# The MLP's down projection: three blocks turned by VectorE and DMA, the fourth summed feature by feature

## The chip, the cores and the metric

The kernel runs on one NeuronCore of a Trainium2 chip. The metric is the device time of one execution in microseconds. The five engines have queues of their own: TensorE (PE in the profile; its weight loads are PEld), VectorE (DVE), ScalarE (ACT), GpSimd (POOL) and SyncE (SP), from whose queue nearly all DMAs are issued.

## The reference, cut to what matters

The model is a decoder of two layers over 256 positions with 2048 features. Each layer has a mixer (dilated attention in layer 0, sparse attention in layer 1), an MLP, and a gated embedding; each works on a normed copy of the residual stream `h` and adds to it. What the change touches is the MLP and the norm that reads its result:

```python
for i in range(DEPTH):
    ...
    hn = rmsnorm(h, mlp_norm_g[i])
    h = h + jnp.square(jax.nn.relu(hn @ mlp_w1[i])) @ mlp_w2[i]
    gate = jax.nn.sigmoid(rmsnorm(h, ple_norm_g[i]) @ ple_w_gate[i])
    h = h + (p[i] @ ple_w_proj[i]) * gate
return rmsnorm(h, final_norm_g)
```

`mlp_w1` is 2048 x 8192 and `mlp_w2` is 8192 x 2048, both float32.

## The kernel before, in words

**Layout.** The residual stream lies in SBUF feature by feature: sixteen tiles `x[k]` of 128 features by 256 tokens, which are the halves of eight tiles `xp[j]` of 128 x 512. Each operand of a product is kept as a rounded part and the rest (`hi`, `lo`), and a product is hi x hi + hi x lo + lo x hi. An activation tile (`xa`, `h`) holds its two parts side by side, 128 x 512.

**Weights come in chunks** of 128 x 1024 float32 (512 KB), one DMA each on SP's queue into one of four `raw` buffers. ScalarE rounds a chunk into `whi` (L227), VectorE subtracts to get `wlo` (L235; six and five buffers), and TensorE uses both. `Program.run` writes this order out: for each chunk it issues the load up to seven chunks ahead, the two splits three to four chunks ahead, then advances every unfinished step by one piece, and then issues the chunk's matmuls. A step is a Python generator; each `yield` puts its next piece behind the next chunk's splits, and `yield "tensor"` behind the next chunk's matmuls. So all engines' queues are fixed in program order.

**Two kinds of product.** `quad` computes four tiles of 128 features, feature by feature: a chunk is 16 matmuls (L366 with 512 columns, weights' rounded part against both parts of the activation; L368 with 256 columns, weights' rest against the rounded part), into four PSUM banks, for which two rings of four (`mm` and `at`) take turns. `token_major` computes 512 features of all tokens, token by token: a chunk is 12 matmuls of 512 columns (L456), into two banks.

**The MLP** (`mlp`) runs over four blocks (`NFB`) of 2048 hidden features. In each, four quads make the hidden tiles `h` (up projection, with the norm's factor, relu and square), then four calls of `token_major`, a quarter (512) of the 2048 output features each, make the block's part of the down projection. `down` sums these parts over the blocks in `y`, token by token: ScalarE copies the first block (L518), VectorE adds the others (L516). After the fourth block's quarter, eight transposes on TensorE (L527) turn the quarter back to feature by feature, in two PSUM banks, behind the next chunk's matmuls; VectorE adds the two banks to `xp` (L531); and `renorm` makes the next norm's activation tiles and its sum of squares.

**After the MLP** comes `ple`: a projection of `p` (one chunk, quad over `pg`), then a quad of the gate over the activation tiles `xa` that `renorm` made, four times in turn. The norm's factor is a hook behind the gate's fifth chunk.

**A bounce** (`bounce`) exists for mixer A: VectorE turns a tile in blocks of 32 x 32 (L867), a DMA writes it to DRAM (L180), and four DMAs read it back with blocks moved (L184), which together is a full transpose; the reads wait for the write on SP's queue.

`add_to_x` adds both halves of a quad's PSUM bank to `x[k]` (L489, L490); `out_proj`, the projection behind each mixer, uses it already.

Of the kernel before, what the change touches and what calls it, by code (L numbers as in the profile page):

```python
# [10 lines left out]
F32 = mybir.dt.float32  # L11
# [4 lines left out]
P = 128  # L16
D = 2048
T = 256
# [10 lines left out]
NFB = 4  # L29
# [9 lines left out]
G_ATTN, G_MLP, G_PLE, G_KV, G_FIN = 0, 2, 4, 6, 7  # L39
# [105 lines left out]
def kernel(ctx: ExitStack, tc: tile.TileContext, a: dict, out: bass.AP):  # L145
    nc = tc.nc
    ctx.enter_context(tc.manual_schedule())
    prog = Program()
# [10 lines left out]
    cur = {}  # L159

    def open_pool(key):
        es = ExitStack()
        cur[key] = es.enter_context(tc.tile_pool(name=key, reuse_waits="tile", bufs=1))
        cur[key + "/es"] = es

    def close_pool(key):
        cur.pop(key)
        cur.pop(key + "/es").close()
# [4 lines left out]
    def bounce(src, name, to):  # L173

        m = src.shape[1] // 4
        d = dpool.tile([P, 4 * m], F32, tag=name, name=name, bufs=2)
        nc.sync.dma_start(d, src)  # L180
        yield
        d4 = d.rearrange("(a s) (b n) -> b s a n", a=4, b=4)
        for b in range(4):
            nc.sync.dma_start(to[32 * b:32 * b + 32], d4[b])  # L184
# [8 lines left out]
    xp = [xg0[:, :2 * T]] + [xpool.tile([P, 2 * T], F32, name=f"x{j}") for j in range(1, KT // 2)]  # L193
# [151 lines left out]
    def renorm(k, gi, to, norm):  # L345

        t = split_hi(k, gi)
        s = norm.square(k)
        yield
        split_lo(t, k, gi)  # L350
        to[k] = t
        norm.add(s)
# [76 lines left out]
    def two_banks(mm):  # L429
        if mm:  # L430
            return [bank(), bank()]
        b = banks2()
        return [b[:, 0, :], b[:, 1, :]]
# [54 lines left out]
    def add_to_x(k, ps):  # L488
        nc.vector.tensor_add(x[k], ps[:, :T], x[k])  # L489
        nc.vector.tensor_add(x[k], ps[:, T:], x[k])  # L490
# [15 lines left out]

    def mlp(layer, xg, norm, to, norm2):

        def down(b, q, ps0, ps1, mm):
            c = slice(q * 512, (q + 1) * 512)  # L510
            if b == q == 0:
                cur["y"] = cur["h"].tile([P, 2, D], F32, name=f"y{layer}")
            y = cur["y"]
            for j, ps in enumerate((ps0, ps1)):
                if b:
                    nc.vector.tensor_add(y[:, j, c], ps, y[:, j, c])  # L516
                else:
                    nc.scalar.copy(y[:, j, c], ps)  # L518
            if b < NFB - 1:
                return  # L520
            yield
            yield "tensor"
            tr = two_banks(not mm)
            for f in range(4):
                for j in range(2):
                    k = 4 * q + f
                    nc.tensor.transpose(tr[f // 2][:, (f % 2 * 2 + j) * P:(f % 2 * 2 + j + 1) * P],  # L527
                                        y[:, j, k * P:(k + 1) * P], ident)
            yield
            for i in range(2):  # L530
                nc.vector.tensor_add(xp[2 * q + i], tr[i], xp[2 * q + i])  # L531
            for i in range(2):
                yield
                both = [renorm(4 * q + 2 * i + f, G_PLE + layer, to, norm2) for f in range(2)]
                for g in both:
                    next(g)
                yield
                for g in both:
                    next(g, None)

        for b in range(NFB):
            h = [None] * 16
            for q in range(4):
                def done(f, ps, q=q, h=h):
                    t = sum_halves(ps)
                    yield
                    while norm.r is None:
                        yield
                    nc.vector.scalar_tensor_tensor(t, t, 0.0, norm.rb, op0=ALU.max, op1=ALU.mult)
                    yield  # L550
                    nc.scalar.activation(t, t, AF.Square)
                    ht = cur["h"].tile([P, 2 * T], F32R, tag="h", name="h", bufs=20)
                    yield from split_to(ht, t)
                    h[4 * q + f] = ht
                base = layer * 128 + (b * 4 + q) * 8
                quad(lambda c, base=base: a["w1"][base + c], KT, xg, done,
                     {4: [norm.factor]} if b == 0 and q == 0 else None, late=True,
                     twos=() if q else (0,) if b else (5,) if layer else ())
            for q in range(4):
                base = layer * 128 + (b * 4 + q) * 8  # L560
                token_major(lambda c, base=base: a["w2"][base + c], h,
                            lambda ps0, ps1, mm, b=b, q=q: down(b, q, ps0, ps1, mm), whole=True)

    def load_p(layer, to):
        for k in range(2):
# [7 lines left out]
    def ple(layer, pg, xg, norm, nxt, norm2, last):  # L573
        pj = [None] * KT
# [158 lines left out]
        for q in range(4):  # L733
            def proj_done(f, ps, q=q):
                s = tmp.tile([P, T], F32, tag="es", name="es", bufs=4)
                nc.scalar.copy(s, ps[:, :T])
                t = cur["h"].tile([P, T], F32, tag="pj", name="pj", bufs=8)
                nc.vector.tensor_add(t, ps[:, T:], s)
                pj[4 * q + f] = t
                return  # L740
                yield
            if q == 3 and last:
                pt = {}

                def pt_done(j, ps):
                    pt[j] = f32(cur["h"].tile([P, 2 * T], F32R, tag="h", name="h", bufs=20))
                    nc.scalar.copy(pt[j], ps)
                    return
                    yield
                parity[0] ^= 1  # L750
                token_major(lambda c: a["w_proj"][layer * 4 + q], pg, pt_done,
                            ring=bank if parity[0] else banks2, kt=2)
                last_quad(pt)
                return
            if q == 2 and last:
                prog.op(load_gain)
            quad(lambda c, q=q: a["w_proj"][layer * 4 + q], 2, pg, proj_done, twos=() if q else (0,))
            hooks = {4: [norm.factor]} if q == 0 else {}
            if q == 3 and not last:
                for c in range(6):  # L760
                    hooks[c] = [lambda k=k: split_x(k, G_KV, nxt) for k in (2 * c, 2 * c + 1)]
            quad(lambda c, q=q: a["w_gate"][layer * 32 + q * 8 + c], KT, xg,
                 lambda f, ps, q=q: gate_done(4 * q + f, ps), hooks)
# [206 lines left out]
    def start1():  # L970
        while x_kv[KT - 1] is None or n_b1.r is None:
            yield
        close_pool("h")
        open_pool("O")
        kvt["o0"] = cur["O"].tile([P, 2 * T], F32R, tag="ob", name="ob", bufs=HB // 2)
        for g in range(GB):
            kvt["k", g] = k_tile()
        open_pool("B")
        pb = cur["B"]
        value_tiles("vs", pb)  # L980
        kvt["vc"] = pb.tile([P, GB * DH], F32R, name="vc")
        nc.gpsimd.memset(f32(kvt["vc"]), 0.0)
        kvt["m0"] = pb.tile([P, P], F32, name="m0")
        kvt["m1"] = pb.tile([P, T], F32, name="m1")
        kvt["mc"] = pb.tile([P, 2, 2, 16], F32, name="mc")
        nc.gpsimd.dma_start(kvt["m0"], a["mB0"])
        nc.gpsimd.dma_start(kvt["m1"], a["mB1"])
        nc.gpsimd.dma_start(kvt["mc"], a["mC"])
        kvt["gs"] = pb.tile([P, 2, 64], F32, name="gs")
        for j in range(2):  # L990
            kvt["pc", j] = pb.tile([P, P], F32R, name=f"pc{j}")
            kvt["pcT", j] = pb.tile([P, T], F32R, name=f"pcT{j}")
            for n in ("pc", "pcT"):
                nc.gpsimd.memset(f32(kvt[n, j]), 0.0)
        for n in ("w2_k", "w2_v"):
            zt[n] = pb.tile([P, 2, DH], F32, name=n)
            nc.gpsimd.dma_start(zt[n], a[n])
        for n in ("rcC", "rcS"):
            zt[n] = pb.tile([64, 32], F32, name=n)
            nc.gpsimd.dma_start(zt[n], a[n])  # L1000
        open_pool("C")
        pc = cur["C"]
        for n in ("rk", "rv"):
            zt[n] = pc.tile([P, GB * T], F32, name=n)
        for j in range(2):
            zt["z", j] = pc.tile([P, 8, 2, GB, 16], F32R, name=f"z{j}")
            nc.gpsimd.memset(f32(zt["z", j]), 0.0)
        for n in ("pe_k", "pe_v"):
            zt[n] = pc.tile([P, 32], F32, name=n)
            nc.gpsimd.dma_start(zt[n], a[n])  # L1010
# [388 lines left out]
    ple(1, p1, x_p1, n_p1, None, n_fin, True)  # L1399

    prog.run(load, copy, sub)
    close_pool("h")


# [108 lines left out]
```

## Time and profile before

| | |
|---|---|
| median of 3 runs | 2495.51 us (2495.19 to 2495.7) |
| the profiled execution: time | 2495.55 us |
| the profiled execution: span from first to last instruction | 2493.8 us |
| mean granted TensorE clock | 0.999 |
| PE / DVE / ACT busy | 2482.9 / 1663.7 / 1345.3 us |
| weight chunks split on VectorE (L235) | 875, of 1.22 us each |
| mean DMA rate | 191 GB/s |

A row of the groups gives a source line, an engine, the operation with what it writes and reads, how often, then busy us and the mean ns of one. A row of the waits gives who waited for whom: us in all, times, and the longest. A row of the chain gives start, length and what ran. "L527" is line 527 of the kernel before; in the changed kernel the lines behind the edit are some 17 higher.

### The profile page before, as it was taken

How to read it: one execution, taken by the hardware profiler on the slowest of the kernel's cores; microseconds unless marked ns; L12 is line 12 of the kernel's file. 1: busy time of each engine (PE TensorE's matmuls, PEld its weight loads, DVE VectorE, ACT ScalarE, POOL GpSimd, SP SyncE). 2: the span in 40 equal slices, each digit the busy share in tenths (PEclk: the TensorE clock that was granted, in tenths of full speed). 3: DMA queues.
4: the chain of work that ended last, by engine and by line, in shares of the span. 5: the costliest groups of instructions: out<-in, count | busy, mean ns of one | idle time of the engine just before them, and what ended most of it. 6: DMA issues, size and time to landing. Idle time of an engine off the chain costs nothing.

```text
span 2493.8 us, 35888 instructions
## 1 busy us (share of the span) xinstructions
PE 2482.9 (100%) x13349; PEld 2138.5 (86%) x13349; DVE 1663.7 (67%) x2818; ACT 1345.3 (54%) x2162; POOL 10.4 (0%) x24
## 2 busy tenths in 40 slices
PE   9999999999999999999999999999999999999998
PEld 8888888888888888888888889988888888888887
DVE  7866686865565565556788989776546556556676
ACT  6444444554454453555665788655545445445465
POOL 0000000000000000000000000000000000000000
PEclk9999999999999999999999999999999999999999
DMA  8566566555556656655565743465555555665553
GB/s 276 193 224 205 194 208 202 178 189 192 194 187 193 194 192 192 191 190 187 187 196 187 254 153 125 142 194 186 194 192 188 194 194 187 194 194 188 185 186 131
DMA packets 136110, 475.80 MB, mean 191 GB/s; under 512 B 15296, under 2 KB 19840, under 8 KB 135936
## 3 DMA queue, kind: packets, MB, share of 16 engines
q1 hardware_dynamic: 134832, 471.66, 58.2%
q8 instruction: 104, 1.70, 0.3%
q0 software_dynamic: 528, 1.07, 0.1%
q10 hardware_dynamic: 576, 0.79, 0.1%
q14 instruction: 70, 0.57, 0.1%
HBM read 467.69 MB, written 5.77 MB: 190 GB/s over the span
## 4 chain that ended last, share of the span: by engine, by line
PE 99%; DMA 0%; ACT 0%; issue 0%; DVE 0%; SPq 0%; ACTq 0%; DVEq 0%
PE mm L366 23%; PE mm L456 18%; PE at L366 17%; PE at L456 17%; PE mm L368 11%; PE at L368 8%; PE at L841 1%; PE at L1348 0%; PE mm L1372 0%; PE mm L1104 0%; PE mm L1105 0%; PE mm L598 0%; PE mm L600 0%; PE mm L599 0%; PE at L1298 0%; DMA raw<-in_w_v 0%
## 5 line engine op out<-in xcount | busy, mean ns | idle before, releaser
L235 DVE TENSOR_TENSOR wlo<-raw,whi 128x1024 fp32r<-128x1024 f32 (+1 forms) x875 | 1065.6, 1219 | 631.6 <-PE at L456 131.5
L227 ACT CAST whi<-raw 128x1024 fp32r<-128x1024 f32 (+1 forms) x875 | 919.1, 1051 | 877.7 <-PE mm L456 198.7
L366 PE MATMUL mm<-xa,whi 128*128 128x512 f32 x2208 | 755.2, 395 | 0.0
L368 PE MATMUL mm<-xa,wlo 128*128 128x256 f32 x2208 | 575.4, 278 | 0.0
L366 PE MATMUL at<-xa,whi 128*128 128x512 f32 x1632 | 568.3, 394 | 0.0
L366 PEld LDWEIGHTS mm<-xa,whi 128*128 128x128 f32 x2208 | 399.3, 188 | 76.1 <-issue 0.4
L368 PE MATMUL at<-xa,wlo 128*128 128x256 f32 x1632 | 453.1, 278 | 0.0
L368 PEld LDWEIGHTS mm<-xa,wlo 128*128 128x128 f32 x2208 | 414.9, 188 | 20.3
L366 PEld LDWEIGHTS at<-xa,whi 128*128 128x128 f32 x1632 | 306.1, 188 | 70.3
L456 PE MATMUL at<-whi,h 128*128 128x512 f32 x1024 | 315.8, 390 | 0.0
L456 PE MATMUL mm<-whi,h 128*128 128x512 f32 x1024 | 315.6, 390 | 0.0
L368 PEld LDWEIGHTS at<-xa,wlo 128*128 128x128 f32 x1632 | 306.7, 188 | 0.1
L456 PEld LDWEIGHTS at<-whi,h 128*128 128x128 f32 x1024 | 192.0, 188 | 39.6
L456 PEld LDWEIGHTS mm<-whi,h 128*128 128x128 f32 x1024 | 191.6, 188 | 39.5
L456 PE MATMUL at<-wlo,h 128*128 128x512 f32 x512 | 199.4, 389 | 0.0
L456 PE MATMUL mm<-wlo,h 128*128 128x512 f32 x512 | 199.3, 389 | 0.0
L456 PEld LDWEIGHTS mm<-wlo,h 128*128 128x128 f32 x512 | 96.1, 188 | 20.0
L456 PEld LDWEIGHTS at<-wlo,h 128*128 128x128 f32 x512 | 96.1, 188 | 19.9
L456 PE MATMUL mm<-whi,xa 128*128 128x512 f32 x320 | 98.9, 390 | 0.0
L374 DVE TENSOR_TENSOR et<-mm,es 128x256 f32<-128x256 f32 x137 | 55.7, 421 | 61.6 <-ACT es L372 59.7
L372 ACT COPY es<-mm 128x256 f32<-128x256 f32 x137 | 48.4, 371 | 68.8 <-PE mm L368 65.8
L456 PEld LDWEIGHTS mm<-whi,xa 128*128 128x128 f32 x320 | 59.7, 188 | 12.2
(331 smaller groups left out, 2131.1 us busy)
## 6 DMA issues: line engine op xcount, KB each, us to landing
raw<-in_w SPq DMA_DIRECT2D x512, 512.0 KB, 3.5
raw<-in_w_qk SPq DMA_DIRECT2D x96, 512.0 KB, 3.6
raw<-in_w_gate SPq DMA_DIRECT2D x64, 512.0 KB, 3.8
raw<-in_w_kv SPq DMA_DIRECT2D x48, 512.0 KB, 4.1
raw<-in_w_v SPq DMA_DIRECT2D x47, 512.0 KB, 4.4
raw<-in_w_q SPq DMA_DIRECT2D x32, 512.0 KB, 4.3
raw<-in_w_oB SPq DMA_DIRECT2D x32, 512.0 KB, 3.5
raw<-in_w_oA SPq DMA_DIRECT2D x16, 512.0 KB, 3.4
```

The source lines that it names most:

```text
L227: nc.scalar.copy(hi[:, c], t[:, c])
L235: nc.vector.tensor_sub(lo[:, c], t[:, c], f32(hi)[:, c])
L366: nc.tensor.matmul(ps, hi[:, col:col + P], rhs, start=first, stop=False)
L368: nc.tensor.matmul(ps[:, :T], lo[:, col:col + P], rhs[:, :T], start=False, stop=last)
L372: nc.scalar.copy(s, ps[:, :T])
L374: nc.vector.tensor_add(t, ps[:, T:], s)
L456: nc.tensor.matmul(st[j], *parts[j][i], start=k == i == 0, stop=k == kt - 1 and i == 2)
L841: nc.tensor.matmul(sb[:, j, T + (g - 1) * P:T + g * P] if g else sb[:, j, :T], q[:, own], k[:, own] if g else k, start=True, stop=True)
```

## The change

The sums of the first three blocks still grow in `y`, which is now two tiles, one for each half of the 2048 features. When the third block's second quarter of a half is added, VectorE turns the half in blocks of 32, one instruction of 128 x 1024 for each 128 tokens, into tiles `z` of a pool of their own. Two DMAs write these to DRAM and eight read them back into a tile `yw`, feature by feature, during the rest of the third block and the fourth block's up projection. Four adds of 128 x 512 on VectorE put the half into `xp`. The fourth block's down projection is four quads, whose results `add_to_x` adds to `x`, and `renorm` follows. The transposes on TensorE and the adds from their banks are gone. The pool `z` is closed behind the MLP, and a pool `j` for the tiles `pj` of `ple` is opened in its place. Both layers are changed alike.

```diff
     def mlp(layer, xg, norm, to, norm2):
+        prog.op(lambda: open_pool("z"))
+        y = {}
+
         def down(b, q, ps0, ps1, mm):
-            c = slice(q * 512, (q + 1) * 512)
-            if b == q == 0:
-                cur["y"] = cur["h"].tile([P, 2, D], F32, name=f"y{layer}")
-            y = cur["y"]
+            half, c = q // 2, slice(q % 2 * 512, (q % 2 + 1) * 512)
+            if b == 0 and q % 2 == 0:
+                y[half] = cur["h"].tile([P, 2, D // 2], F32, tag="y", name="y", bufs=2)
             for j, ps in enumerate((ps0, ps1)):
                 if b:
-                    nc.vector.tensor_add(y[:, j, c], ps, y[:, j, c])
+                    nc.vector.tensor_add(y[half][:, j, c], ps, y[half][:, j, c])
                 else:
-                    nc.scalar.copy(y[:, j, c], ps)
-            if b < NFB - 1:
+                    nc.scalar.copy(y[half][:, j, c], ps)
+            if b < NFB - 2 or q % 2 == 0:
                 return
-            yield
-            yield "tensor"
-            tr = two_banks(not mm)
-            for f in range(4):
-                for j in range(2):
-                    k = 4 * q + f
-                    nc.tensor.transpose(tr[f // 2][:, (f % 2 * 2 + j) * P:(f % 2 * 2 + j + 1) * P],
-                                        y[:, j, k * P:(k + 1) * P], ident)
-            yield
-            for i in range(2):
-                nc.vector.tensor_add(xp[2 * q + i], tr[i], xp[2 * q + i])
-            for i in range(2):
+            zs = []
+            for j in range(2):
                 yield
-                both = [renorm(4 * q + 2 * i + f, G_PLE + layer, to, norm2) for f in range(2)]
-                for g in both:
-                    next(g)
+                z = cur["z"].tile([P, D // 2], F32, tag="z", name="z", bufs=2)
+                nc.vector.transpose(z.rearrange("p (b t r) -> p t b r", b=4, r=32),
+                                    y[half][:, j].rearrange("p (t b s) -> p t b s", b=4, s=32))
+                zs.append(z)
+            w = cur["h"].tile([P, 8, T], F32, tag="y", name="yw", bufs=2)
+            yield
+            moves = [bounce(z, "dM", w[:, 4 * j:4 * j + 4]) for j, z in enumerate(zs)]
+            for g in moves:
+                next(g)
+            for g in moves:
                 yield
-                for g in both:
-                    next(g, None)
+                next(g, None)
+            yield
+            for n in range(4):
+                yield
+                xn = xp[4 * half + n].rearrange("p (f a r) -> p f a r", f=2, r=32)
+                wn = w.rearrange("p a (t r) -> p t a r", r=32)[:, 2 * n:2 * n + 2]
+                nc.vector.tensor_add(xn, wn, xn)
...
             for q in range(4):
                 base = layer * 128 + (b * 4 + q) * 8
-                token_major(lambda c, base=base: a["w2"][base + c], h,
-                            lambda ps0, ps1, mm, b=b, q=q: down(b, q, ps0, ps1, mm), whole=True)
+                if b < NFB - 1:
+                    token_major(lambda c, base=base: a["w2"][base + c], h,
+                                lambda ps0, ps1, mm, b=b, q=q: down(b, q, ps0, ps1, mm), whole=True)
+                    continue
+
+                def done(f, ps, q=q):
+                    add_to_x(4 * q + f, ps)
+                    yield
+                    yield from renorm(4 * q + f, G_PLE + layer, to, norm2)
+                quad(lambda c, base=base: a["w2"][base + c], 16, h, done, late=True)
+        prog.op(lambda: close_pool("z"))
+        prog.op(lambda: open_pool("j"))
...
-                t = cur["h"].tile([P, T], F32, tag="pj", name="pj", bufs=8)
+                t = cur["j"].tile([P, T], F32, tag="pj", name="pj", bufs=8)
...
+        close_pool("j")
         close_pool("h")
```

More of the change, by code (lines that the diff above doesn't have):

```diff
@@ L1401 @@
     prog.run(load, copy, sub)
+    close_pool("j")
     close_pool("h")
```

## The prediction

> **What bounds the kernel now.** I read the head of the page first, then the waits of TensorE, then the chain of waits in order of time.
>
> ```profile
> span 2493.8 us, 35888 instructions
> ...
> PE 2482.9 (100%) x13349; PEld 2138.5 (86%) x13349; DVE 1663.7 (67%) x2818; ACT 1345.3 (54%) x2162; POOL 10.4 (0%) x24
> ...
> PEclk9999999999999999999999999999999999999999
> ...
> PE 99%; DMA 0%; ACT 0%; issue 0%; DVE 0%; SPq 0%; ACTq 0%; DVEq 0%
> ```
>
> TensorE (PE) fills the span, at an even granted clock; the chain that ends last is 99% PE. The waits view with TensorE alone says the same more sharply:
>
> ```profile
> PE mm L772 <- DVE ones L196: 1.1, 1, 1.1
> PE at L273 <- DVE acc L264: 1.0, 1, 1.0
> PE at L456 <- ACT whi L227: 0.5, 2, 0.3
> ```
>
> In the whole run PE waited 2.6 us, in four places. So the time is the sum of what PE issues, and a change counts by what it does to PE's own stream plus any wait that it brings back. VectorE (67%) and ScalarE (54%) matter only if they come so late that PE waits.
>
> **What PE pays for the fourth block now.** The chain in order of time (start, length, what) has the second layer's blocks:
>
> ```profile
> 2004.00 21.76 PE at L456 x96
> 2114.51 21.77 PE mm L456 x96
> ...
> 2290.30 21.77 PE mm L456 x96
> 2312.08 5.44 PE at L456 x24
> 2318.39 16.34 PE at L456 x72
> ```
>
> A quarter of the down projection, token by token, is 96 matmuls of 512 columns in 21.76 us: 227 ns each, 8 chunks of 2.72 us. Between the end of one block's last quarter (2004.00 + 21.76 = 2025.76) and the next block's first (2114.51) lie 88.75 us: the up projection's 4 quads of 8 chunks, feature by feature, so 22.19 us a quad, 2.773 us a chunk of 16 matmuls (8 of 512 and 8 of 256 columns). In the fourth block there is a hole after 24 matmuls: 2312.08 + 5.44 = 2317.52, and the next piece starts at 2318.39. These 0.87 us are the eight transposes of one quarter:
>
> ```profile
> L527 PE MATMUL mm<-ident,y 128*128 128x128 f32 x32 | 4.1, 272 | 0.0
> L527 PE MATMUL at<-ident,y 128*128 128x128 f32 x32 | 4.1, 272 | 0.0
> ```
>
> ```profile
> 2379.89 0.62 PE L366 MATMUL mm<-pg,whi 128*128 128x512 f32 x2
> ...
> 2382.66 0.40 PE L366 MATMUL at<-xa,whi 128*128 128x512 f32 x1
> ...
> 2385.44 1.03 PE L527 MATMUL mm<-ident,y 128*128 128x128 f32 x8
> 2386.23 0.47 PE L366 MATMUL at<-xa,whi 128*128 128x512 f32 x1
> ```
>
> The first pair are two lines of the groups, 64 transposes in all, so 8 groups of 8 over both layers. The second is PE's timeline at the end of the second layer's MLP: the last group, behind the gate's first chunk, holds PE from 2385.44 to 2386.23, 0.79 us, and 0.87 with the slower restart that the hole in the chain includes.
>
> **Part by part. Removed from PE:** 8 groups of transposes, 8 x 0.87 = 6.96 us (8 x 0.79 = 6.3 as the lower bound). They lie on the bound itself, so all of it is gained.
>
> **Changed on PE:** the fourth block's four quarters become quads: 32 chunks a layer at 2.773 instead of 2.72 us, 64 x 0.053 = +3.4 us. The products are the same number of columns (12 x 512 = 8 x 512 + 8 x 256 = 6144); four more matmuls a chunk cost the difference. No quad with h as its moving side is in this trace; the nearest rows are the quads over xa (2.773) and the one over pg, 2382.66 - 2379.89 = 2.77. So the bounds are 0 (the pace of the down projection) and 3.8 us (64 x 0.06); I take 3.4, since two sorts of quads agree.
>
> The Trainium skill, "TensorE: Matmul & The Clock Gate", section Back-to-back issue gap, gives N/2.4 + 2.5 ns between matmuls; by it 512 columns would be 215.8 ns, and the exchange would cost an estimated 0.6 us. The trace disagrees: 227 ns, and 0.053 us a chunk.
>
> **Removed from and added to VectorE.** The groups of its instructions (busy, mean ns):
>
> ```profile
> L235 DVE TENSOR_TENSOR wlo<-raw,whi 128x1024 fp32r<-128x1024 f32 x871 | 1062.9, 1222 | 631.0 <-PE at L456 131.5 <-PE mm L456 130.0 <-PE mm L368 123.7
> ...
> L516 DVE TENSOR_TENSOR y<-mm,y 128x512 f32<-128x512 f32 x24 | 16.5, 692 | 9.1 <-PE mm L456 9.1
> ...
> L867 DVE STREAM_TRANSPOSE zA<-p 128x1024 f32<-128x1024 f32 x7 | 8.7, 1246 | 0.2
> ...
> L489 DVE TENSOR_TENSOR x<-mm,x 128x256 f32<-128x256 f32 x16 | 6.7, 416 | 0.0
> ...
> L531 DVE TENSOR_TENSOR x<-mm,x 128x512 f32<-128x512 f32 x8 | 5.2, 687 | 6.0 <-PE mm L527 6.0
> L799 DVE TENSOR_TENSOR p<-p,oT 128x512 f32<-128x512 f32 x7 | 4.8, 686 | 0.0
> ```
>
> A layer loses 8 sums into y (8 x 0.69 = 5.5 us) and 8 adds of the turned quarter (8 x 0.69 = 5.5). It gains 4 turns of 128x1024 (the turn in mixer A is this very instruction: 4 x 1.25 = 5.0), 8 adds of 512 from the returned tile (8 x 0.69 = 5.5, by the nearest add of two SBUF tiles) and 32 adds of 256 from PSUM (32 x 0.42 = 13.4). Net +12.9 us a layer. Where it lands:
>
> ```profile
> 917.70:1004.70 87.00, 87.00 (x386) 72.12 (x385) 46.65 (x49) 37.38 (x43) 0.00 (x0) 1.00 0.60 193
> 1004.70:1093.50 88.80, 88.80 (x513) 77.66 (x513) 53.26 (x71) 46.49 (x70) 0.00 (x0) 1.00 0.59 190
> 1093.50:1183.30 89.80, 89.80 (x411) 74.64 (x410) 58.69 (x78) 46.17 (x67) 0.00 (x0) 1.00 0.59 188
> ```
>
> These are windows of layer 0: the third block's down projection, the fourth block's up and its down projection (length, then busy PE, PEld, DVE, ACT, POOL; clock, DMA share, GB/s). VectorE is busy 46.65 of 87, 53.26 of 88.8, 58.69 of 89.8 us. With two turns and four adds more (5.2) in each of the first two, and about 58.69 - 11.0 + 13.4 = 61 in the third, it stays under 70%. Cost to the end: nothing, as long as its lead over PE lasts.
>
> That lead:
>
> ```profile
> DVE wlo L235 <- PE at L456: 131.5, 88, 1.8
> ...
> ACT pt L877 <- DMA wA<-dA: 7.7, 7, 1.6
> ```
>
> VectorE keeps waiting for PE to give a wlo buffer back; there are five, so it starts the split of a chunk when four chunks still lie ahead of it: 4 x 2.72 - 1.22 = 9.7 us between a wlo that is ready and PE's use of it. A stall of VectorE under 9.7 us is not seen by PE.
>
> **Added DMAs and waits.** Per half of the features: two writes of 512 KB to DRAM, then eight reads of 128 KB, all on SP's queue between weight loads. Both sorts exist in mixer A; the two lines' answers (with the landing of each) and the weights' row:
>
> ```profile
> L180 SPq DMA_DIRECT2D dA<-zA x7: 326/327/331, 101.6 to 386.9; - x7
> ...
> DMA to landing us min/median/max: 2.6/3.5/5.0
> ```
>
> ```profile
> L184 SPq DMA_DIRECT2D wA<-dA x28: 325/424/852, 104.5 to 393.2; - x28
> ...
> DMA to landing us min/median/max: 2.6/4.0/5.0
> ```
>
> ```profile
> raw<-in_w SPq DMA_DIRECT2D x512, 512.0 KB, 3.5
> ```
>
> Two waits are new. SP's reads wait for the writes to land, and weight loads stand behind them. VectorE's first add of the half waits for the reads, and the splits of weights stand behind that. In the program the first add comes four chunks after the writes, 4 x 2.72 = 10.9 us. The moves take, by the longest landing of each leg in series (write, write, read, read), 4 x 5.0 = 20 us; by room on the queues: 193 GB/s at a share of 0.60 is 322 at full share, 129 to spare, and 2.1 MB there and back take 16 us. So VectorE stands 0 to 9 us at that add, likeliest about 5, against a lead of 9.7: PE waits 0. The two halves are 16 chunks (44 us) apart and VectorE is idle a third of that, so the lead is back before the second. The single bounce in mixer A agrees: its reader waited 7.7 us in seven times, and PE has no row for it.
>
> The Trainium skill, "VectorE: DVE Perf Modes", section Rules for kernel authors, speaks against the change: for a 128x128 transpose it names TensorE, if PSUM will do as the target. Here the trace decides by which engine is full: each turn moved is 0.87 us off PE per 1.25 on an engine that idles a third of the time; kept to the rule, the sum would be +3.4 us for the quads alone.
>
> **The sum.** -6.96 + 3.4 = -3.6 us. The profiled execution took 2495.55 us (span 2493.8 and 1.75 around it); 2492.0 would be its time. The median of the three runs, 2495.51, lies 0.04 below it; so 2491.9 to 2492.0, -0.14%. A measurement of this kernel can tell about 0.2% (5 us) from no change, so this counts as the same.
>
> **Rivals.**
>
> *PSUM comes back late at the gate (same).* Now the last quarter's two banks are read at once; in the changed kernel the last quad fills a ring of four, two features' adds are put off by a chunk, and after one chunk (the projection of p) the gate wants this ring.
>
> ```profile
> 2380.09 1.29 DVE L516 TENSOR_TENSOR y<-at,y 128x512 f32<-128x512 f32 x2 [1.44 <-PE at L456]
> 2381.29 1.22 DVE L235 TENSOR_TENSOR wlo<-raw,whi 128x1024 fp32r<-128x1024 f32 x1
> 2382.42 1.41 DVE L738 TENSOR_TENSOR pj<-mm,es 128x256 f32<-128x256 f32 x4
> ```
>
> VectorE follows PE by 0.20 us here (2379.89 to 2380.09). From the end of the last quad: the first two features' four adds (0.42 each) from -1.39 + 0.2 on, when their half of the chunk is done, over at 0.5; a split, 1.7; the other two features' four adds, 3.4. PE asks for the third bank at 2.77 + 1.39 = 4.2. That is 0.8 us to spare. One split more ahead of them costs 0.4 a layer (2492.8), the four pj adds as well 1.9 (2495.7).
>
> *The bounce outlasts the lead (slower).* It decides from moves of 10.9 + 9.7 = 20.6 us on. Half as long again as 16 us is 24.5: VectorE stands 13.6, PE waits 3.9 in each of four halves, 15.7 us: 2507.7. For it: two bounces at once, in runs of 1 KB, beside full weight traffic, which no row shows. Against it: mixer A's 1.1 us a bounce.
>
> *The quads cost nothing extra (faster).* If the 2.773 belonged to the up projection's busier VectorE and not to its matmuls, the whole 6.96 would be won: 2488.6, -0.28%. The page's gap rule gives nearly this. Against it: the chunk over pg has none of that work and takes 2.77 too.
>
> **Chances.** Forecast 0.78 (its own range 2491.4 to 2493.0, by 6.3 to 7.0 off and 3.4 to 3.8 on), late PSUM 0.07, bounce 0.08, free quads 0.07. Faster: 0.07 and 0.01 for what I have not seen. Slower: 0.08 and 0.01. Same: 0.83. The range leaves out the bounce and the free quads, 0.15; it goes up to the late PSUM's 2495.7, and down to half of the free quads, 2495.5 - 6.96 + 1.7 = 2490.3.
>
> **What would show it.** In the profile after: no transposes between the fourth block's quarters; quads of 22.19 us there, and about 177.5 us from the start of its up projection to the projection of p; a turn of about 1.25 us; PE's waits still under 3 us. A PE row naming wlo with VectorE idle on a DMA from dM would prove the bounce; a PE row naming x at the gate's first chunk, the late PSUM; a fourth-block quad of 21.8, the free quads.

## The result and the profile after

The changed kernel takes 2491.78 us (median of 22 runs, 2491.26 to 2493.05), the kernel before beside it on the same chip 2495.3 (22 runs, 2495.03 to 2495.7). The ratio is 0.9986 [0.998, 0.9992]: 3.5 us less, which by 0.2% counts as the same time. The profiled execution of after is its slowest, 2493.05 us (span 2491.3); where that matters it is said.

The head of the page after, its shares of the chain, and the waits view with TensorE alone (us in total, times, longest):

```profile
span 2491.3 us, 36361 instructions
...
PE 2479.3 (100%) x13541; PEld 2144.3 (86%) x13541; DVE 1682.9 (68%) x2874; ACT 1344.8 (54%) x2162; POOL 10.3 (0%) x24
...
PE 97%; DMA 1%; DVE 1%; ACT 0%; issue 0%; SPq 0%; ACTq 0%; DVEq 0%
```

```profile
PE mm L1139 <- ACT et L1133: 1.1, 1, 1.1
PE mm L789 <- DVE ones L196: 1.1, 1, 1.1
PE at L273 <- DVE acc L264: 1.0, 1, 1.0
PE at L456 <- ACT whi L227: 0.4, 1, 0.4
```

TensorE is as full as before. Of its four rows three stood there before (2.6 us); the first row is new and lies far from the change, in the second layer's compression stage (its matmul starts at 1436.4 us). No row names `wlo`, and none names `x` at the gate.

Now the part that was changed. First the chain of before in order of time (start, length, what): the last quarter of the third block's down projection, and the two matmuls of L297 that stand right ahead of the second projection of p, behind the MLP, in layer 0 and then in layer 1. Below it the same places of after, with the start of the first projection of p (2378.54).

```profile
983.37 21.76 PE at L456 x96
...
1210.04 0.43 PE mm L297 x2
...
2179.80 21.76 PE at L456 x96
...
2406.45 0.43 PE mm L297 x2
```

```profile
983.53 21.76 PE at L456 x96
...
1208.21 0.43 PE mm L297 x2
...
2179.28 21.76 PE at L456 x96
...
2378.54 0.46 PE mm L366 x2
...
2403.97 0.43 PE mm L297 x2
```

From the end of the third block to the second projection of p, before takes 1210.04 - 1005.13 = 204.91 us in layer 0 and 2406.45 - 2201.56 = 204.89 in layer 1; after takes 1208.21 - 1005.29 = 202.92 and 2403.97 - 2201.04 = 202.93. That is -1.99 and -1.96, together -3.95 us. Most of the rest of the difference lies between the two layers: from 1210.04 to 2179.80 before has 969.76 us, and from 1208.21 to 2179.28 after has 971.07. The 1.31 us given back there are the new wait of 1.1 us and little else. The median run is 1.27 us faster than the profiled one; that it lacks most of this wait fits the number, but only the slowest run was profiled, so it is not shown.

VectorE's groups of after (busy us, mean ns, idle before), the two kinds of adds, the sums into `y` and the turns:

```profile
L490 DVE TENSOR_TENSOR x<-mm,x 128x256 f32<-128x256 f32 x32 | 13.6, 425 | 1.1
...
L546 DVE TENSOR_TENSOR x<-yw,x 128x512 f32<-128x512 f32 x16 | 11.0, 687 | 14.6 <-DMA yw<-dM 8.4 <-DMA raw<-in_w 6.1
...
L521 DVE TENSOR_TENSOR y<-mm,y 128x512 f32<-128x512 f32 x16 | 10.8, 690 | 4.5 <-PE mm L456 4.5
...
L530 DVE STREAM_TRANSPOSE z<-y 128x1024 f32<-128x1024 f32 x8 | 9.9, 1237 | 0.0
```

And the three windows of layer 0 that the prediction costed (length, busy PE, PEld, DVE, ACT, POOL, clock, DMA share, GB/s):

```profile
917.70:1004.70 87.00, 87.00 (x387) 72.08 (x386) 50.79 (x56) 37.52 (x43) 0.00 (x0) 1.00 0.68 218
1004.70:1093.50 88.80, 88.80 (x513) 77.63 (x512) 57.13 (x77) 46.16 (x69) 0.00 (x0) 1.00 0.66 214
1093.50:1182.30 88.80, 88.80 (x515) 77.68 (x514) 61.05 (x94) 46.28 (x67) 0.00 (x0) 1.00 0.57 190
```

VectorE went from 46.65, 53.26 and 58.69 us to 50.79, 57.13 and 61.05. The DMA share rose by 0.07 to 0.08 where the moves run. None of it reached TensorE.

The first move in time: SyncE's queue and VectorE's timeline (start, length, instruction, in brackets what it stood for):

```profile
966.89 1.10 SPq L180 DMA_DIRECT2D dM<-z  x2
...
972.48 1.76 SPq L184 DMA_DIRECT2D yw<-dM  x4
...
974.76 1.85 SPq L184 DMA_DIRECT2D yw<-dM  x4
```

```profile
983.07 0.69 DVE L546 TENSOR_TENSOR x<-yw,x 128x512 f32<-128x512 f32 x1 [3.67 <-DMA yw<-dM]
```

From the issue of the writes to the first add are 983.07 - 966.89 = 16.2 us. VectorE stood 3.67 us, with the next split of weights behind it, and TensorE did not notice.

### The profile page after: what moved, and what is told of

Its sections match the earlier page's. It is cut to its first block, busy times and chain, and to the rows that moved or that the text cites. A ratio compares the mean times of both kernels' runs of the same rounds, so it can differ in the third digit from the quotient of the medians.

```text
span 2491.3 us, 36361 instructions
## 1 busy us (share of the span) xinstructions
PE 2479.3 (100%) x13541; PEld 2144.3 (86%) x13541; DVE 1682.9 (68%) x2874; ACT 1344.8 (54%) x2162; POOL 10.3 (0%) x24
## 4 chain that ended last, share of the span: by engine, by line
PE 97%; DMA 1%; DVE 1%; ACT 0%; issue 0%; SPq 0%; ACTq 0%; DVEq 0%
PE mm L366 25%; PE at L366 19%; PE mm L456 15%; PE mm L368 12%; PE at L456 11%; PE at L368 10%; DMA raw<-in_w_kv 1%; PE at L858 1%; DVE wlo L235 1%; PE at L1366 0%; PE mm L1390 0%; PE mm L615 0%; PE mm L617 0%; PE mm L616 0%; PE at L1316 0%
## 5 line engine op out<-in xcount | busy, mean ns | idle before, releaser
L456 PE MATMUL mm<-whi,h 128*128 128x512 f32 x768 | 236.5, 389 | 0.0
L456 PE MATMUL at<-whi,h 128*128 128x512 f32 x768 | 236.4, 389 | 0.0
L456 PEld LDWEIGHTS at<-whi,h 128*128 128x128 f32 x768 | 144.2, 188 | 29.9
L456 PEld LDWEIGHTS mm<-whi,h 128*128 128x128 f32 x768 | 143.7, 188 | 29.8
L456 PE MATMUL mm<-wlo,h 128*128 128x512 f32 x384 | 149.4, 389 | 0.0
L456 PE MATMUL at<-wlo,h 128*128 128x512 f32 x384 | 149.4, 389 | 0.0
L366 PE MATMUL at<-h,whi 128*128 128x512 f32 x256 | 88.9, 394 | 0.0
L366 PE MATMUL mm<-h,whi 128*128 128x512 f32 x256 | 88.9, 394 | 0.0
L456 PEld LDWEIGHTS mm<-wlo,h 128*128 128x128 f32 x384 | 72.1, 188 | 15.0
L456 PEld LDWEIGHTS at<-wlo,h 128*128 128x128 f32 x384 | 72.1, 188 | 15.0
```

The costliest lines, as they stand in the source:

```text
L366: nc.tensor.matmul(ps, hi[:, col:col + P], rhs, start=first, stop=False)
L456: nc.tensor.matmul(st[j], *parts[j][i], start=k == i == 0, stop=k == kt - 1 and i == 2)
```

## The experiments

The theory: the time is TensorE's own stream, transposes taken away and quads put in; the moves and VectorE's extra work cost nothing because VectorE's splits lie some 10 us ahead. The rivals: the moves cost something that the transposes pay for; the two terms have other sizes and meet by chance; the lead or the room at the gate's PSUM is far from its end, or already past it. Where a trace is compared below, "the stretch" is the one measured above, from the end of the third block to the second projection of p: 204.91 and 204.89 us before, 202.92 and 202.93 after.

**No moves.** After without the turns, the DMAs and the adds from `yw`:

```diff
-            if b < NFB - 2 or q % 2 == 0:
-                return
-            zs = []
...
-                nc.vector.tensor_add(xn, wn, xn)
+            return
+            yield
```

> The changed kernel without the turns on VectorE, the DMAs to DRAM and back and the adds from the returned tile (the three blocks' sums never reach x); TensorE's instructions are those of the changed kernel. If the bounce is wholly hidden, as the prediction holds: the changed kernel's 2491.8 us, within 0.5. If the bounce costs TensorE a wait somewhere, also later by a thinner lead: faster than 2491.8 by that wait, 1 us or more.

Measured: 2491.99 us (11 runs, 2491.25 to 2492.49), ratio to before 0.9986 [0.9977, 0.9995], the ratio of after itself. In its trace the stretch takes 202.93 us in both layers (1208.25 - 1005.32 and 2403.07 - 2200.14), as in after to 0.01. 8 turns, 8 writes, 32 reads and 16 adds cost nothing that shows: they are hidden.

**No transposes.** Before without the transposes and the adds of the turned quarters:

```diff
-            tr = two_banks(not mm)
-            for f in range(4):
-                for j in range(2):
...
-                    nc.tensor.transpose(...)
...
-                nc.vector.tensor_add(xp[2 * q + i], tr[i], xp[2 * q + i])
```

> The kernel before without the eight groups of transposes on TensorE and the adds of the turned quarters (the MLP's sum never reaches x); renorm stays. By the prediction's first term (0.87 us a group) 2495.3 - 7.0 = 2488.3; by the pieces of the two traces, where a group with its slow restart costs 0.90, 2488.1. If the transposes were partly covered by something else: 2490 or more.

Measured: 2488.36 us (7 runs, 2488.01 to 2489.24), ratio 0.9972 [0.9961, 0.9983]. That is -6.95 us by the medians. In its trace the stretch takes 201.22 us in both layers, 7.36 less than before in all.

**Quads alone.** Before with the fourth block as quads; TensorE still turns the sums of three blocks, one block earlier:

```diff
-            if b < NFB - 1:
+            if b < NFB - 2:
                 return
...
+                if b < NFB - 1:
+                    token_major(...)
+                    continue
+                def done(f, ps, q=q):
+                    add_to_x(4 * q + f, ps)
+                    yield
+                    yield from renorm(4 * q + f, G_PLE + layer, to, norm2)
+                quad(lambda c, base=base: a["w2"][base + c], 16, h, done, late=True)
```

> One part of the change alone: the fourth block's down projection as quads, while the three blocks' sums are turned by TensorE as before, a block earlier. By the prediction's second term (64 chunks of 0.053 us) 2495.3 + 3.4 = 2498.7. If the quads cost nothing extra: 2495.3. With e2 and the changed kernel this closes the sum: -7.0 and +3.4 should add up to -3.6.

Measured: 2498.72 us (11 runs, 2498.59 to 2499.4), ratio 1.0014 [1.0005, 1.0023], +3.41 us. By the medians the two halves add up: -6.95 + 3.41 = -3.54 against -3.5 for the change. The terms are separate, and each has about its forecast size. That the medians agree to 0.04 us is closer than the traces can bear. Counted from the start of the third block's down projection, since the transposes now lie in it, quads alone takes 1.61 us a layer more than before (for layer 0, 1211.58 - 918.01 = 293.57 against 1210.04 - 918.08 = 291.96), +3.22 in all; with -7.36 that is -4.14, against -3.95 for the change. The difference is a slower last piece of before, 0.11 us a layer, which both runs lack and which is thus counted twice; it is shown below.

**A bounce more.** After with a third 512 KB bounce in each half (of the first tile into itself), four DRAM buffers for it, between the same writes and the same first add:

```diff
-            moves = [bounce(z, "dM", w[:, 4 * j:4 * j + 4]) for j, z in enumerate(zs)]
+            to = [w[:, :4], zs[0].rearrange("p (a n) -> p a n", a=4), w[:, 4:]]
+            moves = [bounce(zs[j], "dM", t) for j, t in zip((0, 0, 1), to)]
```

> The changed kernel with three bounces instead of two per half (the first tile goes to DRAM and back a second time, into a buffer that is no longer needed), between the same writes and the same first add. By the prediction's price for the bounce that outlasts the lead: moves of 24 us, VectorE stands 13, TensorE waits some 3 to 4 us in each of four halves, 2503 to 2508. If the lead is longer than 9.7 us or the DMAs overlap better than the room on the queues says: 2491.8, and VectorE stands under 9 us.

Measured: 2491.82 us (11 runs, 2491.45 to 2492.84), ratio 0.9986. The queue's and VectorE's timeline, then VectorE's wait:

```profile
966.70 2.26 SPq L180 DMA_DIRECT2D dM<-z  x3
```

```profile
987.33 0.69 DVE L548 TENSOR_TENSOR x<-yw,x 128x512 f32<-128x512 f32 x1 [7.82 <-DMA yw<-dM]
```

```profile
DVE x L548 <- DMA yw<-dM: 25.9, 4, 7.8
```

The moves took 987.33 - 966.70 = 20.6 us. The prediction had called 20.6 the point from which TensorE waits, but expected half as many bytes more to take 24.5. The third bounce added 4.4 us, not 8, so the spare room on the queues is not by itself what timed the first two. Part of the room seems to have come from the weights: ScalarE's waits for them (`raw<-in_w`) grew from 33.7 to 51.6 us. VectorE stood 7.8 us, 4.1 more than in after; the smallest lead of a split over the first matmul that uses it was still about 2.4 us (split over at 992.08, matmul at 994.50).

**Two bounces more.** The same with four bounces in each half:

```diff
+            to = [w[:, :4], *(z.rearrange("p (a n) -> p a n", a=4) for z in zs), w[:, 4:]]
+            moves = [bounce(zs[j], "dM", t) for j, t in zip((0, 0, 1, 1), to)]
```

> The changed kernel with four bounces per half (each tile goes to DRAM and back a second time, into buffers that are no longer needed), between the same writes and the same first add. In the changed kernel the moves of a half took 16.2 us from the first write to the first add and VectorE stood 3.7; with three bounces 20.6 and 7.8. One bounce more should make it about 25 and 12, past the lead of 9.8, which by the smallest leads seen (7.1 and about 2.9 us) is used up at a stand of some 10.7. If the lead is what hides the bounce: TensorE waits 1 to 4 us in each of four halves, 2494 to 2508. If something else hides it: 2491.8.

Measured: 2499.44 us (11 runs, 2494.86 to 2503.54), ratio 1.0015 [1.0006, 1.0023]. The waits of TensorE, and of ScalarE and VectorE:

```profile
PE at L368 <- DVE wlo L235: 3.0, 1, 3.0
```

```profile
ACT whi L227 <- DMA raw<-in_w: 88.2, 38, 6.8
...
DVE x L548 <- DMA raw<-in_w: 28.8, 3, 11.2
```

Here the row appears that the prediction named as the bounce's proof: TensorE waits for `wlo`. It comes in one half of the four and not in each, in layer 1; the profiled execution (2497.23 us) is faster than the median, and what the others waited for no trace shows. In that half VectorE's first add starts 26.1 us behind the issue of the writes (2231.95 - 2205.81), after a stand of 11.16 us, and TensorE waits 3.02 us for the split behind it. The profile puts this stand down to a weight load that landed last, and not to `yw`; but SyncE issues the last reads from `dM` only from 2222.59 to 2226.53, and the weight loads behind them. In layer 0's first half the same takes 23.2 us (989.70 - 966.54), and TensorE does not wait. ScalarE waits 88.2 us for weights, where after has 33.7. So the lead is what hides the moves, and it ends between three and four bounces; the change uses two.

The wait costs more than its length: the stretch of layer 1 takes 208.06 us, 5.13 more than in after, for a wait of 3.02. Behind the wait the granted clock is 0.50 (2236 to 2238); the next two experiments show what that costs.

**Adds later.** After with the adds of the fourth block's quads one chunk later:

```diff
                 def done(f, ps, q=q):
+                    yield
                     add_to_x(4 * q + f, ps)
```

> The changed kernel with the fourth block's adds to x put off by one more chunk, to find the room at the gate's PSUM ring. In the changed kernel's trace the last of them ended at 2381.57 us and the gate wants the third bank at 2382.55, 1.0 us to spare. Put off behind one more split and the four adds of the projection of p they end some 4 us later: TensorE waits about 3 us a layer for x at the gate's first chunk, 2497 to 2499. If the ring is not wanted then: 2491.8.

Measured: 2498.66 us (11 runs, 2497.76 to 2502.93), ratio 1.0016 [1.0007, 1.0025]. Its wait of TensorE, and VectorE's timeline of after at the end of layer 1's MLP:

```profile
PE at L366 <- DVE x L490: 5.3, 4, 2.4
```

```profile
2378.78 1.22 DVE L235 TENSOR_TENSOR wlo<-raw,whi 128x1024 fp32r<-128x1024 f32 x1
...
2381.15 0.42 DVE L490 TENSOR_TENSOR x<-at,x 128x256 f32<-128x256 f32 x1
```

And the first matmul of the gate in TensorE's timeline of after:

```profile
2381.16 0.40 PE L366 MATMUL at<-xa,whi 128*128 128x512 f32 x1
```

In after the last add of the fourth block ends at 2381.15 + 0.42 = 2381.57, and the gate's first chunk, which starts at 2381.16, asks for its third bank half a chunk later, at 2381.16 + 1.39 = 2382.55: 1.0 us to spare. One chunk (2.77 us) later is too late by nearly two, and the wait comes in both layers. The room is real and small.

The waits are 2.41 and 0.26 us in layer 0, 2.39 and 0.26 in layer 1; yet the stretch takes 207.98 us in layer 0 and 206.23 in layer 1. The windows behind the longer wait tell the two apart (length, busy PE, PEld, DVE, ACT, POOL, granted clock, DMA share, GB/s):

```profile
1190.40:1193.70 3.30, 3.30 (x12) 2.73 (x11) 2.06 (x4) 2.24 (x5) 0.00 (x0) 0.50 0.04 15
2390.00:2393.30 3.30, 3.30 (x21) 2.90 (x20) 2.02 (x4) 2.15 (x5) 0.00 (x0) 1.00 0.14 57
```

In layer 0 the granted clock is half for these 3.3 us and TensorE does 12 matmuls instead of 21; in layer 1, behind a wait of nearly the same length, it stays whole. That makes most of the 1.75 us between the layers. Against after's 202.9, nearly the same waits cost 5.1 us in one layer and 3.3 in the other.

**All four blocks turned by DMA.** If the quads cost 3.4 us, the fourth block could stay token by token too, each quarter turned by VectorE and one bounce behind it:

```diff
-            if b < NFB - 2 or q % 2 == 0:
+            if b < NFB - 1:
                 return
...
+            z = cur["h"].tile([P, 1024], F32, tag="z", name="z", bufs=1)
+            nc.vector.transpose(...)
+            yield
+            w = cur["h"].tile([P, 4, T], F32, tag="y", name="yw", bufs=4)
+            g = bounce(z, "dM", w)
...
+                token_major(lambda c, base=base: a["w2"][base + c], h,
```

> A version that should beat both: all four blocks' sums stay token by token, and each quarter of the features is turned by VectorE and one bounce behind the fourth block, so neither transposes nor fourth-block quads are left on TensorE. By the two terms of the sum, both taken out: 2495.3 - 7.0 = 2488.3. The gate wants the last quarter at its seventh chunk, about 19.4 us behind the last down product; by one bounce of about 10 us, the adds and renorm it is ready at some 18. If that comes late: 1 to 4 us more a layer, 2490 to 2496, with a wait of TensorE for xa at the gate. (The buffers of the rope's shuffle are one instead of two, for room.)

Measured: 2499.83 us (10 runs, 2498.68 to 2503.45), ratio 1.002 [1.001, 1.0029]. Slower, and by a wait that was not among those expected. TensorE's timeline, with the norm's sum over features (L273) and the second projection of p:

```profile
1205.38 0.50 PE L273 MATMUL mm<-ones,acc 128*128 128x1 f32 x4
...
1211.79 0.79 PE L366 MATMUL mm<-pg,whi 128*128 128x512 f32 x1 [3.71 <-DVE pj L743]
```

The last quarter comes back so late that the sum is taken at 1205.38; in after it is taken at 1199.28, though the down projection of after ends 2.2 us later. On VectorE the work for the factor that comes of this sum now stands ahead of the `pj` adds, and these free the banks that the second projection of p wants: TensorE stands 3.71 us there, in each layer (3.72 in layer 1). That projection takes 7.49 instead of 2.97 us, and the next chunk of the gate 4.58 instead of 2.77, 6.3 us a layer. Only 3.7 of these are the wait. Behind it the granted clock is half, in both layers (2413 to 2417 in layer 1):

```profile
1212.00:1216.00 4.00, 4.00 (x13) 3.42 (x14) 1.95 (x4) 1.32 (x2) 0.00 (x0) 0.50 0.18 70
```

A move that is hidden in mid-stream has no cover at the end of it here.

**Three quarters.** So only the first three quarters of the fourth block are turned whole, and the last stays a quad (its three blocks' sums turned a block earlier; the first line is against the version above, the second against the changed kernel):

```diff
-            if b < NFB - 1:
+            if b < NFB - 1 - (q == 3):
                 return
...
-                if b < NFB - 1:
+                if b < NFB - 1 or q < 3:
                     token_major(...)
```

> All four blocks' sums turned by VectorE and one bounce a quarter for the first three quarters, behind the fourth block; only the last quarter is done as in the changed kernel (three blocks turned early, the fourth a quad with adds to x), so that the norm is complete as early as there. By the two terms: six groups of transposes and the last two are gone (-7.0), two quads instead of eight (+0.85): 2495.3 - 6.1 = 2489.2. If the wait that the version with all quarters turned met (the norm's factor late, so that the second projection of p waits for a PSUM bank) comes from any bounce behind the fourth block and not from the last quarter's alone: 2492 or more. (The returned tile lies in the place of the sums; the rope's shuffle has one buffer.)

Measured: 2491.21 us (11 runs, 2490.87 to 2491.56), ratio 0.9983 [0.9974, 0.9992]. Six quads fewer should have given 2.5 us against after; 0.6 came, and in the stretch (202.93 and 202.68 us) only 0.2. The chain shows the quad behind the down projection, first of this kernel, then of after, each with the first matmul of the quad, some steps of it, and the projection of p behind it:

```profile
1158.93 0.23 PE at L366
...
1159.62 0.24 PE at L366
...
1160.68 0.24 PE at L366
...
1181.53 0.47 PE mm L366 x2
...
1207.82 0.43 PE mm L297 x2
```

```profile
1160.60 0.23 PE at L366
1160.95 0.23 PE at L366
...
1161.98 0.23 PE at L366
...
1182.78 0.46 PE mm L366 x2
```

The same 64 pairs of matmuls take 1181.53 - 1158.93 = 22.60 us here and 1182.78 - 1160.60 = 22.18 in after. Three pairs take 1160.68 - 1159.62 = 1.06 us, against 1161.98 - 1160.95 = 1.03 by the rounded starts of after. The granted clock is 1.00 in both quads. From the projection of p to the second one it is 26.29 us (1207.82 - 1181.53) against 25.43 (1208.21 - 1182.78). Of these 0.86 us about 0.44 are a wait of 0.20 us for `x`, with the slower pairs around it, and the rest is the slower pace again. In layer 1 the quad takes 22.60 us too, and the gate 26.04 (2402.07 - 2376.03): it has the same wait, but behind it the faster pace for a while. So 0.42 + 0.86 + 0.42 + 0.61 = 2.3 us were lost, 0.9 to the waits and 1.4 to a second pace of the same instructions; that is the 2.5 expected less the 0.2 that came.

**The quad entered in pairs.** The same kernel with the last quad's first chunk issued two by two:

```diff
-                quad(lambda c, base=base: a["w2"][base + c], 16, h, done, late=True)
+                quad(lambda c, base=base: a["w2"][base + c], 16, h, done, late=True, twos=(0,))
```

> The three-quarter version with one edit: the first chunk of the last quarter's quad issues its matmuls two by two (two of 512 columns, then two of 256), as the up projection's first quad does behind a down projection. In the version without it this quad took 22.60 instead of 22.19 us and the gate behind it 14.57 and 8.57 instead of 13.87 and 8.41: every third pair took 10 ns longer, from the first chunk on. If this pace is set by the order at the switch from 12 matmuls a chunk to 16, the edit sets it right: 0.4 + 0.4 to 0.8 us a layer less, 2489.2 to 2489.6. If it comes from the DMAs or VectorE's load at that place: 2491.2 again.

Measured: 2490.68 us (11 runs, 2490.14 to 2491.0), before beside it 2495.25, ratio 0.9981 [0.9972, 0.999]. That lies between the two values expected. The quad is back at 22.19 us in both layers; the gate behind it is not, and layer 0's timeline shows where it falls into the slow pace:

```profile
1185.37 0.47 PE L366 MATMUL at<-xa,whi 128*128 128x512 f32 x1 [0.28 <-DVE x L490]
...
1185.80 0.40 PE L366 MATMUL at<-xa,whi 128*128 128x512 f32 x1
...
1186.86 0.40 PE L366 MATMUL at<-xa,whi 128*128 128x512 f32 x1
```

Behind a wait of 0.28 us for `x`, three pairs take 1186.86 - 1185.80 = 1.06 us, ahead of it 1.04. In layer 1 the wait is as long (0.28), and behind it three pairs still take 1.04. This is the fastest version run, 1.1 us under after and with runs that don't overlap its runs; by 0.2% it is still the same time.

**The old pools.** The new wait in the compression stage (L1139, 1.1 us) might come of the pools `z` and `j`, which move tiles about. The kernel without the moves, with the pools of before:

```diff
-        prog.op(lambda: open_pool("z"))
...
-                t = cur["j"].tile([P, T], F32, tag="pj", name="pj", bufs=8)
+                t = cur["h"].tile([P, T], F32, tag="pj", name="pj", bufs=8)
```

> As the run without the moves, but with the pools of before (no pool z, the tiles pj back in the pool h). In the changed kernel and in the run without moves TensorE waited 0.2 to 1.2 us for the compression's activation in the key stage of layer 1, where weights are ready only 2 to 4 us ahead; in the kernels with the old pools it did not. If the new pools' places in SBUF cause this: 2491.3 to 2491.5, and a spread as narrow as before's 0.7. If it is only where the stage falls in time: 2491.8 to 2492.0, with the same spread.

Measured: 2491.61 us (11 runs, 2491.36 to 2492.38), ratio 0.9986, between the two values expected, and the wait is there:

```profile
PE mm L1114 <- ACT et L1108: 0.8, 1, 0.8
```

Not the pools, then; nor the moves, since these are left out here and the wait stays. The wait is in the profiled executions of after, of the kernels with no, three and four bounces, of the later adds and of all four blocks turned (0.2 to 1.5 us), and not in those of before, no transposes, quads alone and the two three-quarter kernels. What brings it is open.

## Why the prediction was right

It said 2492.0 us, and -3.6 us; it came to 2491.78, and -3.5.

*Transposes, -6.96.* No transposes gave -6.95 by the medians and -7.36 in the trace. The price of 0.87 us a group, with the slower restart that the hole in the chain contains, was the right one, a little low, and not the lower bound of 0.79.

*Quads, +3.4.* Quads alone gave +3.41, so quads over `h` run like those over `xa`: from the end of the third block's down projection (2201.04) to the projection of p (2378.54) are 177.50 us, as forecast, eight quads of 22.19. The free quads are out. The gap rule of the Trainium skill, "TensorE: Matmul & The Clock Gate", section Back-to-back issue gap, would have made 0.6 us of this by the prediction's estimate; the run has 3.41, and the measurement decides. That section gives the rule for a matmul by itself and not for a stream of them, which the prediction did not say.

*VectorE's work.* Turns 1237 ns (forecast 1.25 us), adds 687 and 425 ns (0.69 and 0.42), busy time in the three windows 50.79, 57.13 and 61.05 us (51.9, 58.5 and 61). Hidden, as the run without the moves shows (202.93 us in the stretch, with them and without).

The other advice that the prediction weighed, that of the Trainium skill, "VectorE: DVE Perf Modes", section Rules for kernel authors, for transposes on TensorE, did not pay here, where TensorE is the full engine: keeping the transposes while changing the rest took +3.41 us instead of -3.5.

*Moves, 16 us; VectorE stands about 5, TensorE 0.* Measured 16.2 us, 3.67 us in that half and 4.8 at the longest of the four halves. The figure agreed, the working behind it only in part, so its closeness is partly luck. The 16 us were worked out from the room on the queues, and by that a half more would take 24.5; it took 20.6. The spare room alone is not what times two bounces; what does is open. VectorE also came to the add 12.5 us behind the writes (983.07 - 3.67 - 966.89), where the prediction had 10.9. The rival was therefore priced too dear (TensorE waiting 3.9 us a half at three bounces, and 0 measured) and its point of decision was too early: at 20.6 us the lead was still 2.4, at 23.2 TensorE did not wait, and at 26.1 it waited 3.0, so the point lies near 23 us. On the other hand the price counted a wait at its length, and with four bounces 3.02 us of waiting cost 5.13. The mechanism was right, as four bounces show.

*Late PSUM, 0.8 us to spare.* Measured 1.0, and past it with the adds a chunk later. It was the tightest place of the change, as supposed.

*What the sum did not have.* The MLPs gained 3.95 us, not 3.56. Two causes appear in the rows. Behind each hole of transposes the other 72 matmuls took 16.34 to 16.35 us in before's chain, and three quarters of 21.76 are 16.32: 0.02 to 0.03 in three places a layer. And before ran its last steps up to the second projection of p at the slower pace that the experiments met later, after not. The two chains behind the norm's factor, before and then after:

```profile
2401.49 0.24 PE at L366
...
2402.55 0.24 PE at L366
```

```profile
2400.15 0.23 PE at L366
...
2401.19 0.23 PE at L366
```

Three pairs, 1.06 and 1.04 us; over 16 pairs that is 0.11 us a layer. Both together make 2 x (0.11 + 0.08) = 0.38. About as much is given back in the median run (-3.95 to -3.5), and the wait for `et` in the compression stage is the one place found for it. So the total agreed within 0.1 us in part by luck: two small things, which the sum had not, cancelled. And the range's lower end does not follow from its own bounds: 7.0 off and 3.4 on 2495.5 give 2491.9 and not 2491.4, and the measured 2491.78 lies 0.1 below that.

## What to carry to other kernels

When one engine fills the span, price a change by that engine's own instructions, each from a row with its restart in it, and test the two terms apart; here their medians added up to within 0.04 us, and their traces to within 0.2. Work moved to other engines and queues is free only as long as the lead of what it delays and the room of the buffers it holds: count both in microseconds before, and find by doubling the moves or delaying them a step how near the end is. If a wait of the full engine does come, look at the granted clock behind it before taking the wait's length for its price: here 3.7 us of waiting cost 6.3. A long move that is hidden in mid-stream need not be hidden at the end of a stage, where the next stage needs its last piece.

## What the runs showed of the hardware that was not expected

The same alternation of 512- and 256-column matmuls has two steady paces, 1.04 and 1.06 us for three pairs (22.19 and 22.60 us a quad), at the same granted clock (1.00 in both quads' windows). For the last quad, the order of its first chunk decided: straight behind a token-by-token product it was slow in both layers, and with that chunk in pairs it was fast in both. Behind a short pause the runs show no rule. Behind the wait for `x` at the gate the pace was slow in layer 0 and fast in layer 1, both with three quarters and with the pairs; behind the norm's sum it turned slow in before and stayed fast in after. What in TensorE does this no run shows.

A wait of TensorE can halve its granted clock for a while after. Behind waits of 3.71 and 3.72 us (all turned) it was 0.50 and a pair took 0.64 instead of 0.35 us; behind 3.02 us (two bounces more) it was 0.50 from 2236 to 2238; behind 2.41 us (adds later) it was 0.50 in layer 0, and behind 2.39 us in layer 1 it stayed 1.00. What decides between the last two no run shows.

A third bounce of 512 KB there and back, beside the same weight traffic, added 4.4 us where the first two took 16.2.
